# A list scheduler's cost table for TensorE turns and engine overlap is replaced, and the first merge of a block inverse is written for both halves alternately

## The chip, the cores and the metric

The kernel runs on one core of a Trainium2 chip. Its engines are PE (matmul; PEld is its weight load), DVE (vector), ACT (scalar), POOL (GpSimd) and SP (which issues most of the DMAs). They run at the same time; each takes its own instructions strictly in the order in which they stand in its queue. The metric is the device time of one execution in microseconds; the median of three runs before the change is 2573.09 us (2571.34 to 2573.66).

## The reference

One layer of a hybrid decoder, 1024 tokens of width 1024, all in fp32:

```python
x = x + 0.5 * swiglu(rmsnorm(x, ffn1_norm), ffn1_w_gate, ffn1_w_up, ffn1_w_down)
h = rmsnorm(x, mix_norm)
x = x + hybrid_mixer(h, pos, w_in, ...)
x = x + 0.5 * swiglu(rmsnorm(x, ffn2_norm), ffn2_w_gate, ffn2_w_up, ffn2_w_down)
return rmsnorm(x, final_norm)
```

The mixer multiplies `h` by one wide matrix `w_in` and feeds two branches. Branch A is causal dilated sliding-window attention, three groups of four heads with 64 channels, whose outputs are mixed by a softmax over the groups' log-denominators. Branch B is a gated delta rule with eight heads of 128 channels: a short causal convolution and silu on q, k and v, then in chunks

```python
M = where(tri_strict, einsum('bhnid,bhnjd->bhnij', kbeta, kc) * decay, 0.0)
A = M + eye(C)
sol = triangular_solve(A, rhs, left_side=True, lower=True, unit_diagonal=True)
```

and a scan over the chunks that carries a state. Both branches are gated by sigmoids, summed and multiplied by `w_out`.

## The kernel before, in words

**The products.** A wide product is made of three matmuls on operands that are split into a high and a low part of type fp32r (`ff_split`, lines 207 to 218: ACT rounds the high part, L216, and DVE subtracts, L217). These matmuls have 512 (or 256, 272) columns; they are L161 (`proj`, the mixer's projections and the output projection), L274 and L404 (the feed-forward's first half, by a seven-product scheme), L584 (its second half), L697, L801 and L1381. The rest of PE's work is narrow. Transposes through an identity are L201, L877, L928, L975, L1154 and L1226. Full fp32 products, each of which the profile records as two matmuls, are L885, L1129 and the scan's L1185 to L1205. The attention's scores (L864) have 64 rows: the two heads of a pair sit in the upper and the lower half of the array. The smallest are the merges of the triangular inverse, 32 by 32 (L1070, L1075) and 64 by 64 (L1083, L1090).

**The stages.** First feed-forward (to about 715 us), attention (718 to 1046), the combination of the three attention groups mixed with the beginning of head 0 (`combine`, lines 899 to 931, on ACT and DVE, with two transposes L928 for each of eight token tiles and their copy L930), the eight heads of the delta rule (to 1694), the output projection, the second feed-forward and the last norm.

**A head of branch B.** `gdn_keys` projects and convolves k and q (copy out of PSUM L955, convolution L963 on ACT and L965 on DVE, silu L966), and builds the triangular matrix N. `gdn_inverse_blocks` inverts its 32 by 32 diagonal blocks row by row on DVE (L1036 to L1042). `gdn_merge` (from line 1053) joins them: first two 32-blocks into a 64-block, in both halves of the partitions (`quads`: rows 0 to 63 and 64 to 127), over the eight chunks `c`; then two 64-blocks into one of 128. Each join is a product N x T (L1070, L1083), a copy out of PSUM to `W`, and a product U x W (L1075, L1090). `gdn_scan` then runs the eight chunks in turn. Between all of that stand projections of later heads and of the gates, which need nothing of the scan: they are what PE has to fill waits with. Their results leave PSUM through ACT (L942, L955, L828); they have two PSUM buffers (`mm`).

**The end.** The last product of the second feed-forward leaves four PSUM tiles. DVE adds each to its token row (`e4`, L619, tile `acc`), ACT sums the squares (L186), DVE takes the inverse root in twelve small steps that each wait for the one before (`rsqrt_cols`, L123 to L130; tiles `rnv`, `rny`, `rnt`) and writes the row in two halves (L1487, tile `y`), and SP stores them (L1488).

**What sets the order.** The program is built twice. From the first build, `arrange` (from line 1710) simulates the five queues with estimated costs and lays down an order for each; the second build follows it. An instruction's rank is the longest chain of costs behind it. At each step the queue that is free first takes, among the instructions that are ready, the one with the highest rank. `cost` gives for each instruction the time that its queue is held and the time until its result is there; `hop` adds the way from one engine to another. On PE, `form` sorts matmuls into kinds (R wide, T transpose, F full fp32, S scores, Q small squares), and `turn` charges what a change of kind costs. PE goes on with the instruction that follows the last one in program order (`follow`) as long as its rank is within `STAY` of the best.

Of the kernel before, what the change touches and what calls it, by code (L numbers as in the profile page):

```python
# [1055 lines left out]
def gdn_merge(C, N, Tm, Um):  # L1056
# [9 lines left out]
    ps = psum(C, "tM")  # L1066
    W = C.gd.tile([P, NT, 32], F32, name="W", tag="W", bufs=2)
    for lo, hi in quads:
        for c in range(NT):
            nc.tensor.matmul(ps[hi, c * 32:c * 32 + 32], N[lo, c, hi], Tm[lo, c, lo], start=True, stop=True)  # L1070
        nc.vector.tensor_copy(W[hi], ps[hi, :256].rearrange("p (c t) -> p c t", t=32))
    ps = psum(C, "tM")
    for lo, hi in quads:
        for c in range(NT):
            nc.tensor.matmul(ps[hi, c * 32:c * 32 + 32], Um[hi, c, hi], W[hi, c, :], start=True, stop=True)  # L1075
        nc.vector.tensor_copy(Tm[hi, :, lo], ps[hi, :256].rearrange("p (c t) -> p c t", t=32))
        nc.vector.transpose(Um[lo, :, hi], Tm[hi, :, lo])
# [440 lines left out]
class Program:  # L1518
# [118 lines left out]
    def form(self, i):  # L1637
        aps = [a for a in i["ins"] if a["kind"] == "physical_ap"]
        if i["engine"] == "PE":
            if aps[0]["dtype"] == "float32r":  # L1640
                return "R"
            if i.get("is_transpose"):
                return "T"
            return "F" if aps[0]["ap"][0][1] > 64 else "S" if i["outs"][0]["ap"][0][1] > 64 else "Q"
        if i["engine"] == "Activation":
            return {"Exp": "E", "Silu": "U", "Sigmoid": "G", "Ln": "L"}.get(str(i.get("func")).split(".")[-1], "")
        return ""

    def turn(self, a, b, n):

        if a == b:
            return 0
        if b == "S" or b == "Q" or a == "Q":
            return (200 if n < 256 else 300) if a == "S" else 93
        if a == "S":
            return 200 if n < 256 else 300
        return -80 if b == "R" and a in "TF" else 6

# [8 lines left out]
    def cost(self, k):  # L1667
# [15 lines left out]
        if q == 0:  # L1683
            t = {"R": n / 2.4 + 13, "T": 109, "F": 223, "S": 7, "Q": 117 if n > 32 else 63}[self.kind[k]]
            return t, t + 190 + (300 if self.kind[k] == "S" else 0)
        ps = any(self.place[a["memref"]][0] == "PSUM" for a in aps)
# [14 lines left out]
        else:  # L1701
            t = 100 + 0.9 * n + (80 if i["opcode"] == "TensorScalarAffineSelect" else 0)
        return t, t


BACKLOG = 4000
STAY = 1000


# [4 lines left out]
def arrange(prog, pools):  # L1714
# [15 lines left out]
    while stack:  # L1730
        k = stack.pop()
        rank[k] = cost[k][1] if k < n else 0.0
        for c, whole in kids[k]:
            rank[k] = max(rank[k], rank[c] + (cost[k][1] + hop(p.queue[k], p.queue[c]) if whole else 0))
# [21 lines left out]
    while count < n:  # L1756
# [20 lines left out]
        if q == 0 and last[0] is not None:  # L1777
            f = follow.get(last[0])
            if f is not None and not taken[f] and not left[f] and ready[f] <= t and rank[f] >= rank[k] - STAY:
                k = f  # L1780
# [14 lines left out]
        if q == 0:  # L1795
            free0 = clock[q]
            clock[q] -= 80 if p.kind[k] in "TF" else 0
        end = t + cost[k][1]
# [7 lines left out]
        while todo:  # L1806
# [4 lines left out]
            elif not whole:  # L1811
                at = clock[q] if p.queue[c] == q else t
            elif p.queue[c] == q and not p.dma[k]:
                at = clock[q]
            else:
                at = end + hop(q, p.queue[c])
# [51 lines left out]
```

## Time and profile before

| | |
|---|---|
| median of 3 runs | 2573.09 us |
| profiled execution, its own time | 2572.86 us |
| its span, first to last instruction | 2571.1 us |
| granted TensorE clock, mean | 0.991 |
| PE busy | 2508.9 us, 98% |
| DVE busy | 1825.5 us, 71% |
| ACT busy | 983.8 us, 38% |
| PE's share of the chain that ended last | 90% |

How to read the lines that follow. A row of a timeline has the start and the duration in microseconds, the engine, the line, the operation, the tile written and the tiles read, the shapes, and the count of instructions that it merges; in brackets stands how long the engine was idle before and who released it. Matmuls are pipelined, so a row's duration overlaps the next row; what a product costs is the distance between two starts. A row of the waits has the idle time in total, the number of times and the longest one.

### The profile page before, as it was taken

What the parts mean: (1) busy time and instruction counts of PE and PEld (TensorE: products, weight loads), DVE (VectorE), ACT (ScalarE), POOL (GpSimd) and SP (SyncE); (2) the same over time, 40 slices, a digit from 0 to 9 for tenths busy, and PEclk for the clock granted to TensorE, in tenths of its full rate; (3) what the DMA queues carried; (4) which work ended last, traced back from release to release, by engine and by line L of the source; (5) the groups of instructions that cost most, each with busy time, mean ns of one, the idle gap of its engine ahead of it and who ended that gap; (6) DMA issues with size and microseconds to landing.
All of it is one profiled execution on the core that took longest, in us unless ns stands there. A gap on an engine that the chain in (4) does not pass through costs nothing.

```text
span 2571.1 us, 34921 instructions
## 1 busy us (share of the span) xinstructions
PE 2508.9 (98%) x12739; PEld 2074.0 (81%) x12739; DVE 1825.5 (71%) x4059; ACT 983.8 (38%) x1899; POOL 24.4 (1%) x36
## 2 busy tenths in 40 slices
PE   7999999999999999899999999989999999999996
PEld 7788888888888877688888888868888888888885
DVE  8867666768744455888888888546668766667578
ACT  4422332444422336333443335254443333333443
POOL 0000000000000000000000000000000000000000
PEclk9999999999999999999999999999999999999998
DMA  4233224836343331322222213255542223328453
GB/s 159 80 115 114 99 96 168 289 109 203 118 123 94 93 82 52 91 66 64 56 62 56 68 48 81 66 184 193 182 137 91 106 91 115 115 98 301 138 168 111
DMA packets 258172, 301.06 MB, mean 117 GB/s; under 512 B 41840, under 2 KB 175184, under 8 KB 258000
## 3 DMA queue, kind: packets, MB, share of 16 engines
q1 hardware_dynamic: 255696, 292.54, 34.8%
q10 hardware_dynamic: 2304, 6.29, 1.0%
q8 instruction: 100, 1.64, 0.3%
q14 instruction: 72, 0.59, 0.1%
HBM read 217.34 MB, written 75.14 MB: 114 GB/s over the span
## 4 chain that ended last, share of the span: by engine, by line
PE 90%; DVE 6%; DMA 2%; ACT 1%; issue 1%; SPq 0%; DVEq 0%; ACTq 0%
PE mm L161 22%; PE tC L404 13%; PE mm L404 8%; PE tM L404 8%; PE mm L584 4%; PE tC L584 4%; PE tA L161 3%; PE tM L584 3%; PE tA L584 3%; PE mm L697 2%; PE mm L274 2%; PE tC L274 2%; PE tC L1381 2%; PE mm L1381 2%; DMA sgl<-sgbd 1%; PE tA L885 1%
## 5 line engine op out<-in xcount | busy, mean ns | idle before, releaser
L216 ACT CAST fH<-fraw 128x512 fp32r<-128x512 f32 x482 | 289.1, 620 | 463.6 <-PE tM L404 89.4
L217 DVE TENSOR_TENSOR fL<-fraw,fH 128x512 fp32r<-128x512 f32 x482 | 323.0, 689 | 123.8 <-ACT fH L216 118.9
L161 PE MATMUL mm<-hH,fH 128*128 128x512 f32 x896 | 361.5, 410 | 8.7 <-ACT xp L955 5.0
L161 PE MATMUL mm<-hH,fL 128*128 128x512 f32 x896 | 361.0, 405 | 0.0
L161 PE MATMUL mm<-hL,fH 128*128 128x512 f32 x896 | 360.3, 404 | 0.0
L161 PEld LDWEIGHTS mm<-hH,fH 128*128 128x128 f32 x896 | 169.9, 190 | 43.4 <-ACT xp L955 6.2
L161 PEld LDWEIGHTS mm<-hH,fL 128*128 128x128 f32 x896 | 169.7, 190 | 33.3 <-issue 2.3
L161 PEld LDWEIGHTS mm<-hL,fH 128*128 128x128 f32 x896 | 170.1, 190 | 30.3 <-issue 1.7
L404 PE MATMUL mm<-hL,fH 128*128 128x512 f32 x320 | 124.5, 389 | 0.0
L404 PE MATMUL mm<-hH,fL 128*128 128x512 f32 x320 | 121.2, 389 | 0.1
L404 PE MATMUL mm<-hH,fH 128*128 128x512 f32 x320 | 119.0, 389 | 0.0
L576 ACT CAST fH<-hid 128x512 fp32r<-128x512 f32 x154 | 95.0, 617 | 53.1 <-DMA hid<-hd1x 15.8
L577 DVE TENSOR_TENSOR hid<-hid,fH 128x512 fp32r<-128x512 f32 x154 | 104.5, 685 | 5.5 <-ACT fH L576 5.5
L438 DVE TENSOR_TENSOR e<-tM,e 128x512 f32<-128x512 f32 x40 | 26.1, 687 | 79.0 <-PE tM L404 79.0
L216 ACT CAST fH<-hH 128x512 fp32r<-128x512 f32 x68 | 42.3, 622 | 91.3 <-PE tC L584 33.3
L867 DVE CUSTOM_DVE_ANT_0 s<-tC,masks 128x128 f32<-128x128 f32 (+1 forms) x96 | 30.4, 350 | 58.4 <-PE tC L864 35.1
L404 PEld LDWEIGHTS mm<-hH,fL 128*128 128x128 f32 x320 | 60.1, 188 | 13.0 <-DVE fL L217 0.5
L965 DVE SCALAR_TENSOR_TENSOR ka<-xp,cw,ka 128x512 f32<-128x512 f32 x96 | 69.4, 757 | 1.3 <-ACT ka L963 0.8
L404 PEld LDWEIGHTS mm<-hH,fH 128*128 128x128 f32 x320 | 60.0, 188 | 12.6 <-ACT e L408 0.2
L404 PEld LDWEIGHTS mm<-hL,fH 128*128 128x128 f32 x320 | 60.1, 188 | 12.4
L584 PE MATMUL tC<-fH 128*128 128x512 f32 x176 | 68.4, 390 | 0.0
L584 PE MATMUL tC<-fL,fH 128*128 128x512 f32 x176 | 68.2, 389 | 0.0
(402 smaller groups left out, 6200.4 us busy)
## 6 DMA issues: line engine op xcount, KB each, us to landing
fraw<-in_w_in_dram SPq DMA_DIRECT2D x66, 512.0 KB, 3.8
fraw<-in_ffn_w_gate_dram SPq DMA_DIRECT2D x22, 1024.0 KB, 5.2
fraw<-in_ffn_w_up_dram SPq DMA_DIRECT2D x22, 1024.0 KB, 7.2
hL<-in_ffn_w_down_dram SPq DMA_DIRECT2D x8, 1024.0 KB, 6.3
fraw<-in_ffn_w_down_dram SPq DMA_DIRECT2D x8, 1024.0 KB, 6.1
fraw<-in_w_branch_b_dram SPq DMA_DIRECT2D x8, 1024.0 KB, 5.6
fraw<-in_w_out_dram SPq DMA_DIRECT2D x8, 1024.0 KB, 7.3
vb<-xp ACTq DMA_DIRECT2D x48, 128.0 KB, 2.4
```

The source lines that it names most:

```text
L161: nc.tensor.matmul(ps, w, x, start=k == 0 and i == 0, stop=k == kt - 1 and i == 2)
L216: nc.scalar.copy(h, src)
L217: nc.vector.tensor_tensor(out=l, in0=src, in1=h.bitcast(F32), op=ALU.subtract)
L274: nc.tensor.matmul(ps[:, n0:n0 + n], w, x[:, k, c], start=k == 0 and i == 0, stop=k == KT - 1 and i == 2)
L404: nc.tensor.matmul(ps, w, x, start=opens and k == 0 and q == 0, stop=k == 3 and q == 2, skip_group_check=True)
L576: C.nc.scalar.copy(h, v.bitcast(F32))
L577: C.nc.vector.tensor_tensor(out=v, in0=v.bitcast(F32), in1=h.bitcast(F32), op=ALU.subtract)
L584: self.C.nc.tensor.matmul(ps, x[:, m], w, start=p == 0 and i == 0, stop=p == NPAIR - 1 and i == 2)
L697: nc.tensor.matmul(ps[:, :n], h[:, k, b * P:b * P + P], W[k][w], start=k == 0 and i == 0, stop=k == KT - 1 and i == 2)
L867: nc.vector.tensor_tensor_reduce(s[:, h, :nk], ps[h][:, :nk], mask, 1.0, NEG, op0=ALU.add, op1=ALU.max, accum_out=o[:, 128 + h:129 + h])
L965: nc.vector.scalar_tensor_tensor(o, x, w, o, op0=ALU.mult, op1=ALU.add)
L1381: nc.tensor.matmul(ps, mx[:, c], W[k][w], start=i == 0, stop=i == len(seq) - 1)
```

## The change

Three things change; no arithmetic does.

The loops of the first merge in `gdn_merge` are turned: the products of both halves are written alternately over the chunks, all sixteen into the same PSUM tile as before, and the two copies (and the transposes) follow them.

```diff
     ps = psum(C, "tM")
     W = C.gd.tile([P, NT, 32], F32, name="W", tag="W", bufs=2)
+    for c in range(NT):
+        for lo, hi in quads:
+            nc.tensor.matmul(ps[hi, c * 32:c * 32 + 32], N[lo, c, hi], Tm[lo, c, lo], start=True, stop=True)
     for lo, hi in quads:
-        for c in range(NT):
-            nc.tensor.matmul(ps[hi, c * 32:c * 32 + 32], N[lo, c, hi], Tm[lo, c, lo], start=True, stop=True)
         nc.vector.tensor_copy(W[hi], ps[hi, :256].rearrange("p (c t) -> p c t", t=32))
     ps = psum(C, "tM")
+    for c in range(NT):
+        for lo, hi in quads:
+            nc.tensor.matmul(ps[hi, c * 32:c * 32 + 32], Um[hi, c, hi], W[hi, c, :], start=True, stop=True)
     for lo, hi in quads:
-        for c in range(NT):
-            nc.tensor.matmul(ps[hi, c * 32:c * 32 + 32], Um[hi, c, hi], W[hi, c, :], start=True, stop=True)
         nc.vector.tensor_copy(Tm[hi, :, lo], ps[hi, :256].rearrange("p (c t) -> p c t", t=32))
         nc.vector.transpose(Um[lo, :, hi], Tm[hi, :, lo])
```

The scheduler's costs change. The scores get two kinds, S for the upper half and s for the lower, of which the second costs nothing extra behind the first; the table of turns is new; an instruction of DVE or ACT holds its queue 82 or 100 ns less than its result takes, and one that needs the result of another on the same queue waits 40 ns more.

```diff
-        if b == "S" or b == "Q" or a == "Q":
-            return (200 if n < 256 else 300) if a == "S" else 93
-        if a == "S":
-            return 200 if n < 256 else 300
-        return -80 if b == "R" and a in "TF" else 6
+        t = (205 if n < 256 else 305) if a == "S" else 260 if b == "s" else 0
+        if b in "SsQ":
+            return t + (0 if a in "Ss" else 93)
+        if a in "SsQ":
+            return t + (135 if b == "R" else 55) + (100 if a == "Q" else 0)
+        return t + (36 if b == "R" else 9)
...
-        return t, t
+        return t - (0, 82, 100, 0)[q], t
```

And PE stays longer with what it does. Behind a narrow product it goes on with narrow ones up to a difference in rank of `LINGER`, behind a wide one with wide ones up to `STAY`, and takes any of the same sort if the one that follows in program order isn't ready.

```diff
+LINGER = 3000
...
-            if f is not None and not taken[f] and not left[f] and ready[f] <= t and rank[f] >= rank[k] - STAY:
+            wide = p.kind[last[0]] == "R"
+            if f is None or taken[f] or left[f] or ready[f] > t:
+                f = None
+            if f is None or (p.kind[f] == "R") != wide:
+                alike = [(r, c) for r, c in now[0] if not taken[c] and (p.kind[c] == "R") == wide]
+                f = min(alike)[1] if alike else f
+            if f is not None and rank[f] >= rank[k] - (STAY if wide else LINGER):
                 k = f
```

Behind line 1066 the lines of the changed kernel lie two further on: L1075 becomes L1076 (its loops are turned as well), L1083 becomes L1085, L1487 becomes L1489. The new order reaches every queue. On PE, the 11692 matmuls are the same; runs of narrow products between wide ones fall from 462 to 313. The places that matter are shown in the prediction.

More of the change, by code (lines that the diff above doesn't have):

```diff
@@ L1643, in form @@
                 return "T"
-            return "F" if aps[0]["ap"][0][1] > 64 else "S" if i["outs"][0]["ap"][0][1] > 64 else "Q"
+            return "F" if aps[0]["ap"][0][1] > 64 else "Q" if i["outs"][0]["ap"][0][1] <= 64 else "s" if aps[0]["offset"] >= 64 * aps[0]["ap"][0][0] else "S"
         if i["engine"] == "Activation":
@@ L1649, in turn @@
     def turn(self, a, b, n):
-        if a == b:
+        if a == b or a + b == "Ss":
             return 0
-        if b == "S" or b == "Q" or a == "Q":
-            return (200 if n < 256 else 300) if a == "S" else 93
-        if a == "S":
-            return 200 if n < 256 else 300
-        return -80 if b == "R" and a in "TF" else 6
+        t = (205 if n < 256 else 305) if a == "S" else 260 if b == "s" else 0
[4 more added lines that the diff above has]
+        return t + (36 if b == "R" else 9)
     def run(self, a):
@@ L1683, in cost @@
         if q == 0:
-            t = {"R": n / 2.4 + 13, "T": 109, "F": 223, "S": 7, "Q": 117 if n > 32 else 63}[self.kind[k]]
-            return t, t + 190 + (300 if self.kind[k] == "S" else 0)
+            t = {"R": n / 2.4 + 13, "T": 109, "F": 223, "S": n * 0.83 + 106, "s": n * 0.83 + 106, "Q": 117 if n > 32 else 63}[self.kind[k]]
+            return t, t + 190
         ps = any(self.place[a["memref"]][0] == "PSUM" for a in aps)
@@ L1733, in arrange @@
         for c, whole in kids[k]:
-            rank[k] = max(rank[k], rank[c] + (cost[k][1] + hop(p.queue[k], p.queue[c]) if whole else 0))
+            if whole:
+                near = p.queue[k] == p.queue[c] and not p.dma[k]
+                step = cost[k][1] + (hop(p.queue[k], p.queue[c]) if not near else 40 if p.queue[k] in (1, 2) else 0)
+                rank[k] = max(rank[k], rank[c] + (cost[k][0] if near and not p.queue[k] else step))
+            else:
+                rank[k] = max(rank[k], rank[c])
         for d in list(full[k]) + list(after[k]):
@@ L1796, in arrange @@
             free0 = clock[q]
-            clock[q] -= 80 if p.kind[k] in "TF" else 0
         end = t + cost[k][1]
@@ L1813, in arrange @@
             elif p.queue[c] == q and not p.dma[k]:
-                at = clock[q]
+                at = end + 40 if q in (1, 2) else clock[q]
             else:
```

## The prediction

> **What bounds the kernel now.** I read the page, then the busy times by stage, then what the matmul engine PE waits for.
>
> ```profile
> span 2571.1 us, 34921 instructions
> PE 2508.9 (98%) x12739; PEld 2074.0 (81%) x12739; DVE 1825.5 (71%) x4059; ACT 983.8 (38%) x1899; POOL 24.4 (1%) x36
> ```
>
> PE works in 98% of the span, so what counts is what its products cost and where it still waits. The stages of the mixer (attention, combine, eight heads):
>
> ```profile
> 718.00:1046.00 328.00, 326.75 (x1863) 265.03 (x1864) 167.87 (x464) 127.92 (x365) 3.03 (x4) 0.99 0.30 82
> 1046.00:1104.00 58.00, 48.11 (x209) 37.87 (x208) 50.88 (x168) 20.47 (x41) 0.43 (x1) 0.91 0.38 101
> 1104.00:1694.00 590.00, 588.01 (x3623) 485.90 (x3621) 479.53 (x1361) 230.12 (x451) 19.75 (x26) 1.00 0.23 65
> ```
>
> The columns are length, then busy time of PE, weight load, DVE, ACT, POOL, then granted clock. Only in the combine stretch does PE fall short (48.1 of 58.0 us, clock 0.91), and there DVE is 88% busy. In the heads PE is full and DVE 81% busy. PE's waits:
>
> ```profile
> PE tA L201 <- DVE rnv L123: 11.6, 2, 9.5
> PE mm L161 <- ACT yaH L166: 9.7, 1, 9.7
> PE mm L161 <- ACT xp L955: 5.0, 2, 4.9
> PE tA L928 <- DVE cM L916: 2.6, 1, 2.6
> PE tA L928 <- DVE cy L925: 2.4, 2, 2.1
> PE tC L1193 <- DVE xp L952: 1.8, 3, 1.0
> ```
>
> The first stands at the kernel's start, the second where the mixer's buffers turn into those of the output projection, three in the combine, the last in the heads. So a change of order can gain on PE in two ways: cheaper neighbours while it is busy, and shorter waits. A third place is the end, where DVE works alone.
>
> **The change part by part.** The new cost table makes the list scheduler write another order on every queue; the merge's loops are turned. No operation is added or removed. I price neighbours on PE by start-to-start times and count them in the two orders.
>
> *Score products (L864).* They use half the rows of the array; the two heads of a block use different halves. Rows of PE:
>
> ```profile
> 814.67 0.39 PE L161 MATMUL mm<-hL,fH 128*128 128x512 f32 x1
> 814.90 0.40 PE L161 MATMUL mm<-hH,fL 128*128 128x512 f32 x1
> 815.23 0.70 PE L864 MATMUL tC<-ka 64*128 64x256 f32 x4
> 815.86 0.50 PE L161 MATMUL mm<-hL,fH 128*128 128x512 f32 x1
> 816.20 0.39 PE L161 MATMUL mm<-hH,fL 128*128 128x512 f32 x1
> ...
> 816.98 0.70 PE L864 MATMUL tC<-ka 64*128 64x256 f32 x2
> 817.61 0.50 PE L161 MATMUL mm<-hH,fL 128*128 128x512 f32 x1
> ```
>
> A wide product takes 0.23 (814.67 to 814.90). A pair of heads (x4, since each fp32 product has two records) takes 0.63, with 0.10 lost on the way in and 0.11 on the way out: 0.84. A lone head takes the same 0.63 and the same 0.21. Before, 16 heads stand alone among 96, after none: eight visits fewer. Four have 256 columns (0.84); four have 128, which lie between half that and all of it, and I take 0.63: 4 x 0.84 + 4 x 0.63 = **5.9 us**.
>
> *The first merge (L1070, L1075; L1076 after).* On PE, at the merge of head 0 (tM is a PSUM tile, ka here the head's matrix N, Tm and U the inverse blocks, W the first products copied out), before:
>
> ```order
> L1154 MATMUL tA<-ident,vT 128x128 x3
> L1070 MATMUL tM<-Tm,ka 32x32 x8
> L1004 MATMUL tA<-seg,strictR 128x512 x2
> L1154 MATMUL tA<-ident,vT 128x128
> L161 MATMUL mm<-hL_5719,fH 128x512
> L161 MATMUL mm<-hH_5717,fL 128x512
> L161 MATMUL mm<-hH_5718,fH 128x512
> L1070 MATMUL tM<-Tm,ka 32x32 x4
> L1075 MATMUL tM<-W,U 32x32 x8
> L1070 MATMUL tM<-Tm,ka 32x32 x4
> ```
>
> and at the same merge now:
>
> ```order
> L161 MATMUL mm<-hL_5719,fH 128x512
> L1070 MATMUL tM<-Tm,ka 32x32 x16
> L161 MATMUL mm<-hH_5717,fL 128x512
> L161 MATMUL mm<-hH_5717,fH 128x512
> L161 MATMUL mm<-hL_5719,fH 128x512
> L1076 MATMUL tM<-W,U 32x32
> L161 MATMUL mm<-hH_5717,fL 128x512
> L1076 MATMUL tM<-W,U 32x32 x15
> ```
>
> Sixteen products, alternating between two parts of the array, now stand together, where eight of one half and four of the other stood apart. Price of a visit, and of neighbours on different parts:
>
> ```profile
> 1182.33 0.39 PE L161 MATMUL mm<-hL,fH 128*128 128x512 f32 x1
> 1182.65 0.69 PE L1070 MATMUL tM<-Tm,ka 32*32 32x32 f32 x16
> 1183.27 0.50 PE L161 MATMUL mm<-hH,fL 128*128 128x512 f32 x1
> 1183.60 0.40 PE L161 MATMUL mm<-hH,fH 128*128 128x512 f32 x1
> ```
>
> Eight products take 0.62, about 0.063 each and 0.11 around them; the wide neighbours lose 0.09 and 0.10. A visit costs some 0.30 beyond its products. All small square products stand in 76 runs before and 62 after: 14 x 0.30 = **4.2 us**.
>
> ```profile
> 1117.14 0.27 PE L1083 MATMUL tM<-Tm,ka 64*64 64x64 f32 x1
> 1117.15 0.27 PE L1090 MATMUL tM<-U,W 64*64 64x64 f32 x1
> ...
> 1117.76 0.44 PE L975 MATMUL tA<-ident,ka 128*128 128x128 f32 x2
> ```
>
> ```profile
> 1278.68 0.68 PE L1090 MATMUL tM<-U,W 64*64 64x64 f32 x8
> 1279.29 0.50 PE L161 MATMUL mm<-hH,fL 128*128 128x512 f32 x1
> ```
>
> Four products of L1090 alone take 0.61; the four with one of L1083 on another part take 0.62. The second part works for nothing. So of two alternating 32-wide products one is free: 0.031 per neighbour. 228 neighbours alternate after, 23 before: 228 x 0.031 = 7.1. What the 23 bring already:
>
> ```profile
> 1108.15 0.34 PE L1070 MATMUL tM<-Tm,ka 32*32 32x32 f32 x5
> ...
> 1109.07 0.50 PE L161 MATMUL mm<-hH,fL 128*128 128x512 f32 x1
> ```
>
> Here 16 products with two changes of part take 0.92 instead of 16 x 0.063 + 0.11 = 1.12: 0.10 a change, 2.3 in all. Net **4.8 us**. These rows show products that write different PSUM tiles; the alternating ones share one. That is not seen, so the bounds are 7.1 (all free) and -2.3 (none), and I take the first less what is had: the 64-wide rows are the nearest.
>
> The Trainium skill, "TensorEngine Tiling (Array Packing)", section "Restrictions and Gotchas", speaks against this: different row tiles cannot access one PSUM bank at the same time. By it the term is -2.3, and the sum 7 us smaller. That is a rival below.
>
> The cost of the turned loops: the first copy out of PSUM now waits for 16 products instead of 8, and behind it on DVE everything queues. The wide products of L161 cover it on PE (the heads' row has 2 us of idle in 590); uncovered it would be 0.5 us twice a head, 8 us.
>
> *Transposes and full fp32 products.*
>
> ```profile
> 640.43 0.39 PE L584 MATMUL mm<-fL,fH 128*128 128x512 f32 x1
> 640.66 0.60 PE L201 MATMUL tA<-ident,xg 128*128 128x128 f32 x4
> ...
> 641.33 0.40 PE L584 MATMUL tC<-fL,fH 128*128 128x512 f32 x1
> ```
>
> From 640.43 to 641.33 stand two wide products (0.46) and four transposes (0.11 each): a visit costs nearly nothing, 0.01 to 0.02. Their runs fall from 417 to 327: **1.6 us**. PE's busy part together: 5.9 + 4.2 + 4.8 + 1.6 = 16.5.
>
> *Combine.* On ACT, between the copies of the combined attention rows (yT, L930); xp are projections copied out of PE's two mm banks, vT and ka what the convolution makes of them, ce softmax weights. Before:
>
> ```order
> L930 COPY yT<-tA 128x256
> L963 ACTIVATE vT<-xp,cw 128x512 x2
> L930 COPY yT<-tA 128x256
> L966 ACT_TABLE_LOAD
> L966 ACTIVATE vT<-vT 128x512
> L955 COPY xp<-mm 128x512 x2
> ```
>
> and now:
>
> ```order
> L963 ACTIVATE vT<-xp,cw 128x512 x2
> L930 COPY yT<-tA 128x256
> L216 CAST fH<-fraw 128x512
> L913 ACTIVATE ce<-ce 128x12
> L966 ACT_TABLE_LOAD
> L966 ACTIVATE vT<-vT 128x512 x2
> L955 COPY xp<-mm 128x512 x2
> L963 ACTIVATE ka<-xp,cw 128x512 x2
> L930 COPY yT<-tA 128x256
> ```
>
> The copies of L955 that free PE's banks still stand behind an activation that waits for DVE. But between the eight visits of L928 PE's order had 3, 13, 16, 20, 10, 9+0 and 109 wide products, and has 4, 16, 21, 21, 28, 11 and 29 now: never two visits without cover. Before, the waits are 10 us, and the clock falls behind the longest:
>
> ```profile
> 1074.71 0.79 PE L161 MATMUL mm<-hH,fH 128*128 128x512 f32 x1 [4.86 <-ACT xp L955]
> 1075.30 0.63 PE L161 MATMUL mm<-hL,fH 128*128 128x512 f32 x1
> 1075.73 0.63 PE L161 MATMUL mm<-hH,fL 128*128 128x512 f32 x1
> ```
>
> There a wide product takes 0.43 instead of 0.23, until about 1079: 3.5 us. So 13.5 us can go. The Trainium skill, "TensorE: Matmul & The Clock Gate", Part 1, has the clock halved after an idle window of about 3.4 us; the 4.86 agrees, and by it waits in shorter pieces cost only themselves. If every wait slowed the clock once more, the term would be 3.5 smaller, which its lower bound holds. But from the second visit to the last DVE's new order holds, with durations of its rows of before, between 31 us (each overlaps its neighbour) and 46 us (none does) of work, and PE only some 31. Taking DVE at 38, PE still waits 7 us, in pieces, and 2 for ACT. I take **4.5 us** of gain, with bounds of -3 and +12.
>
> *The end.* DVE's last rows; acc are the last four token rows, y the output, the others the norm's chain. Before:
>
> ```order
> L619 SCALAR_TENSOR_TENSOR acc_22018<-tC_22650,acc_22018 128x512
> L130 SCALAR_TENSOR_TENSOR rny_22897<-rnt_22898,rny_22897 128x1
> L128 TENSOR_TENSOR rnt_22898<-rny_22897 128x1
> L129 SCALAR_TENSOR_TENSOR rnt_22898<-rnt_22898,rnv_22896 128x1
> ```
>
> and now:
>
> ```order
> L619 SCALAR_TENSOR_TENSOR acc_22018<-tC_22650,acc_22018 128x512
> L129 SCALAR_TENSOR_TENSOR rnt_22862<-rnt_22862,rnv_22860 128x1
> L130 SCALAR_TENSOR_TENSOR rny_22861<-rnt_22862,rny_22861 128x1
> L128 TENSOR_TENSOR rnt_22862<-rny_22861 128x1
> L129 SCALAR_TENSOR_TENSOR rnt_22862<-rnt_22862,rnv_22860 128x1
> ```
>
> The last sum stood in the third token's chain and stands in the second's (22860). On PE the first of the four groups ended 13 products before the last one, and now ends 33 before, 7.5 us.
>
> ```profile
> 2551.00 0.39 PE L584 MATMUL tC<-fH,hid 128*128 128x512 f32 x1
> 2551.39 0.14 DVE L123 TENSOR_SCALAR rnv<-ssq 128x1 f32<-128x1 f32 x1
> 2553.69 1.41 DVE L1487 SCALAR_TENSOR_TENSOR y<-acc,rny,gB 128x512 f32<-128x512 f32 x2
> 2555.03 0.15 DVE L123 TENSOR_SCALAR rnv<-ssq 128x1 f32<-128x1 f32 x1
> 2565.45 2.73 DVE L1487 SCALAR_TENSOR_TENSOR y<-acc,rny,gB 128x512 f32<-128x512 f32 x4
> ```
>
> A chain takes 2.30 (2551.39 to 2553.69), its y 1.34. Before, four chains and all y follow the last product; DVE ends at 2568.18, 17.2 after it, and the store takes 2.9. Now one chain is done by then and half the next: left are the sum (0.6), five steps (1.0), y (1.3) and two chains with y (7.3), about 11 with the 0.7 until DVE takes the sum. Gain **6.2 us**, bounds 3 and 7.
>
> *Elsewhere.* SP loads three x tiles ahead of the first gate weights, and PE starts with 24 transposes instead of 16: earlier transposes, later weights; 0, bounds of 3 either way in the start's 11.6. At the output projection SP's order is the same (heads' last store, then yal), so the 9.7 stays. The feed-forward stages keep their wide products back to back: 0.
>
> **The rivals.** (A) One PSUM tile cannot be written from two parts at once; the halves take turns: 2546 + 7 = 2553. For it: the rule above, and no row with a shared tile; against: the halves write different partitions. (B) DVE binds: PE's gain in the heads (about 9 us of small products, at 81% DVE) comes back as waits like L1193's, 1 us a head, and the combine gains nothing: 2546 + 8 + 4.5 = 2558.5. Against: the order keeps the cover between the steps of the scan. (C) On the other side: each change of part within a shared tile empties the array, as a visit does with 0.10 and 0.11: 228 x 0.2 = 46, and the 4.8 are gone: 2597, slower. It decides from 0.10 a change. Against: at 1108.15 changes save time. (D) The new turns are no better for the chip than the old, and PE's 16.5 and the combine's 4.5 come to nothing: 2567.
>
> **How the numbers follow.** 16.5 + 4.5 + 6.2 = 27.2. The profiled execution took 2572.86 us, span 2571.1 with 1.8 around it; the median is 2573.09. Forecast 2573.1 - 27.2 = 2546. Chances: forecast 0.58, A 0.20, B 0.13, C 0.04, D 0.05. A measurement of this kernel can tell 0.2% (5.1 us) from no change. Low end: the combine gains 12 and the start 2 (2537); high end: B with a little more (2560). Faster: all but C and some of D: 0.93; same 0.03; slower 0.04.
>
> **What would show it.** Right: L864 only as x4; the x32 records of L1070 in some 0.62 us, not 1.1; waits of L928 and L955 down by a third at least; 14 us, not 20, between the last product and the end. Wrong: alternating rows 0.063 apart (A) or further (C); PE waits of over 10 us in the heads (B); a wait at the start above 15.

## The result and the profile after

| | before | after |
|---|---|---|
| median of 4 runs | 2573.38 us | 2559.51 us |
| profiled execution | 2572.86 us | 2555.95 us |
| its span | 2571.1 us | 2554.2 us |

The ratio is 0.9945 with a 95% interval of 0.9928 to 0.9962: 14 us faster, where 27 were forecast. The direction was right; the time lies inside the stated range, half a microsecond from its upper end. The profiled execution of the changed kernel is the quickest of its four (the others took 2558.8 to 2560.7), and 16.9 us are to be accounted for in it. One execution of no_overlap (below) took 5962 us and is marked slow; without it that kernel's median would be 2583.5 us instead of 2584.0.

The head of the page of the changed kernel, its span and the busy times:

```profile
span 2554.2 us, 34905 instructions
PE 2495.8 (98%) x12739; PEld 2070.5 (81%) x12739; DVE 1771.3 (69%) x4059; ACT 980.0 (38%) x1899; POOL 24.6 (1%) x36
```

PE's share is 98% as before, so the share tells nothing of what was won and lost. The busy times of the combine (first to last L928) and of the heads (to the last head's last transposes), in the columns of the prediction:

```profile
1019.80:1056.50 36.70, 33.24 (x153) 26.23 (x153) 33.49 (x141) 19.56 (x38) 0.00 (x0) 1.00 0.44 125
1056.50:1688.20 631.70, 617.47 (x3768) 508.42 (x3765) 477.36 (x1402) 241.88 (x465) 20.84 (x27) 1.00 0.23 64
```

Where PE was idle for 9.9 of 58.0 us in the combine (1046 to 1104 before) it is now idle for 3.5 of 36.7, at the full clock. In the heads, where it was idle for 2 us in 590, it now is for 14.2 in 631.7. PE's waits in the heads (total, times, longest):

```profile
PE tM L1092 <- DVE W L1087: 3.3, 6, 0.8
PE tM L1085 <- DVE Tm L1078: 2.4, 5, 0.8
PE tC L1187 <- DVE S L1203: 1.8, 3, 0.8
PE tA L1004 <- DVE seg L991: 1.4, 3, 1.1
PE tM L1076 <- issue: 1.1, 2, 0.7
PE tM L1076 <- DVE W L1072: 0.8, 2, 0.5
```

They are new, many and short, none above 1.1 us, and most end with an answer of DVE: between the steps of the merges (L1076, L1085, L1092) and in the scan (L1187).

To see both sides I priced every product of both orders by the prediction's distances (a wide product 0.227, a transpose 0.109, a visit to the small ones 0.30, an alternating neighbour 0.031 less, and so on), summed that for each stage, and set it against the stage's length in the trace. What is left over is the stage's excess: its waits, and the slow steps behind them, where the granted clock is halved. The excess is more than the idle time shown. At the entry to attention two rows of PE are

```profile
714.42 0.39 PE L161 MATMUL mm<-hH,fL 128*128 128x512 f32 x1
716.43 0.50 PE L161 MATMUL mm<-hH,fH 128*128 128x512 f32 x1 [1.63 <-ACT xp L828]
```

2.01 us between the starts are 1.78 more than a wide product, and 1.63 is shown as idle, since a matmul's end is modelled. 0.15 a wait matters where waits are short: in the heads the excess is twice the idle time.

| us | before | after | gain |
|---|---|---|---|
| price of all products | 2487.3 | 2468.9 | 18.4 |
| excess: combine | 13.6 | 4.8 | 8.8 |
| excess: heads | 8.3 | 28.9 | -20.6 |
| excess: entry to attention | 6.6 | 2.1 | 4.5 |
| first product, and excess of the first 100 us | 22.1 | 19.8 | 2.3 |
| excess: attention, output projection, feed-forwards | 13.2 | 16.1 | -2.9 |
| from the last product's start to the end | 20.1 | 13.6 | 6.5 |
| span | 2571.1 | 2554.2 | 16.9 |

(The rows are rounded. The prices are estimates from the prediction's rows, so the split between price and excess is one too.) By these prices PE's products became as much cheaper as forecast and a little more, the end and the combine gained, and the heads gave 20.6 us back.

### The profile page after: what moved, and what is told of

The parts are those of the page before. It is cut to its first block, busy times and chain, and to the rows that moved or that the text cites. A ratio compares the mean times of both kernels' runs of the same rounds, so it can differ in the third digit from the quotient of the medians.

```text
span 2554.2 us, 34905 instructions
## 1 busy us (share of the span) xinstructions
PE 2495.8 (98%) x12739; PEld 2070.5 (81%) x12739; DVE 1771.3 (69%) x4059; ACT 980.0 (38%) x1899; POOL 24.6 (1%) x36
## 4 chain that ended last, share of the span: by engine, by line
PE 85%; DVE 9%; DMA 3%; issue 1%; ACT 1%; SPq 1%; ACTq 0%; DVEq 0%
PE mm L161 18%; PE tC L404 13%; PE mm L404 9%; PE tM L404 8%; PE mm L584 5%; PE tC L584 4%; PE tM L584 4%; PE tA L584 4%; PE tA L161 3%; PE mm L697 2%; PE mm L274 2%; PE tC L274 2%; PE tC L161 2%; PE mm L1383 2%; PE tC L1383 1%; DVE ka L965 1%
## 5 line engine op out<-in xcount | busy, mean ns | idle before, releaser
L161 PE MATMUL mm<-hH,fH 128*128 128x512 f32 x896 | 360.2, 403 | 4.1 <-ACT gt L942 1.6
L161 PE MATMUL mm<-hL,fH 128*128 128x512 f32 x896 | 357.8, 400 | 0.0
L161 PE MATMUL mm<-hH,fL 128*128 128x512 f32 x896 | 352.6, 400 | 0.1
L161 PEld LDWEIGHTS mm<-hH,fH 128*128 128x128 f32 x896 | 168.9, 189 | 37.8 <-ACT gt L942 2.1
L161 PEld LDWEIGHTS mm<-hH,fL 128*128 128x128 f32 x896 | 169.1, 189 | 33.4 <-issue 1.0
L161 PEld LDWEIGHTS mm<-hL,fH 128*128 128x128 f32 x896 | 169.3, 189 | 29.4
L404 PE MATMUL mm<-hH,fL 128*128 128x512 f32 x320 | 123.7, 389 | 0.0
L576 ACT CAST fH<-hid 128x512 fp32r<-128x512 f32 x154 | 94.9, 616 | 14.8 <-DMA hid<-hd1x 9.4
L965 DVE SCALAR_TENSOR_TENSOR ka<-xp,cw,ka 128x512 f32<-128x512 f32 x96 | 74.6, 785 | 17.5 <-ACT ka L963 16.7
L431 DVE TENSOR_TENSOR e<-tC,e 128x512 f32<-128x512 f32 x40 | 27.3, 686 | 66.9 <-PE tC L404 66.9
L584 PE MATMUL mm<-fL,fH 128*128 128x512 f32 x176 | 68.4, 390 | 0.0
```

Of the source, the lines that this page charges most:

```text
L161: nc.tensor.matmul(ps, w, x, start=k == 0 and i == 0, stop=k == kt - 1 and i == 2)
L404: nc.tensor.matmul(ps, w, x, start=opens and k == 0 and q == 0, stop=k == 3 and q == 2, skip_group_check=True)
L431: tt(out=p1[i], in0=ps, in1=p1[i], op=ALU.add)
L576: C.nc.scalar.copy(h, v.bitcast(F32))
L584: self.C.nc.tensor.matmul(ps, x[:, m], w, start=p == 0 and i == 0, stop=p == NPAIR - 1 and i == 2)
L965: nc.vector.scalar_tensor_tensor(o, x, w, o, op0=ALU.mult, op1=ALU.add)
```

## The experiments

Each kernel ran four or five times, merge_only eleven times. The table puts them together; price and excess are as above, from each run's profile. The last column is how many us of the heads had a granted TensorE clock of one half, by the clock records of that trace. "Stay" is the stay rule, "turned" the turned loops, "overlap" the terms of 82, 100 and 40 ns (see overlap_only for what else it holds there), "prices" the costs and turns on PE.

| kernel | what it has of the change | median us | ratio to before, 95% | price | heads' excess | half clock |
|---|---|---|---|---|---|---|
| after_again | all | 2559.3 | 0.9939 (0.9925 to 0.9952) | 2468.9 | 30.7 | 10.2 |
| halves_apart | all, halves unmixed within the order | 2559.3 | 0.9943 (0.9930 to 0.9955) | 2476.0 | 25.1 | 6.8 |
| sched_only | all but turned | 2559.0 | 0.9936 (0.9924 to 0.9949) | 2475.3 | 23.4 | 6.8 |
| old_stay | all but stay | 2562.5 | 0.9953 (0.9941 to 0.9966) | 2468.7 | 34.8 | 17.1 |
| old_turn | all but prices | 2547.5 | 0.9899 (0.9886 to 0.9913) | 2469.8 | 18.6 | 0 |
| no_overlap | all but overlap | 2584.0 | 1.0038 (1.0025 to 1.0052) | 2466.1 | 53.0 | 56.2 |
| overlap_only | overlap | 2543.3 | 0.9883 (0.9870 to 0.9897) | 2475.5 | 12.0 | 0 |
| merge_only | turned | 2573.7 | 1.0000 (0.9991 to 1.0009) | 2482.2 | 15.0 | 3.4 |
| overlap_turn | overlap, prices | 2561.1 | 0.9954 (0.9940 to 0.9967) | 2475.3 | 27.1 | 6.8 |
| overlap_stay | overlap, stay | 2551.0 | 0.9914 (0.9900 to 0.9928) | 2475.2 | 16.8 | 6.8 |
| old_turn_stay | overlap, turned | 2550.1 | 0.9913 (0.9899 to 0.9926) | 2468.7 | 25.4 | 17.1 |
| turn_zero | all, turns at nothing | 2541.5 | 0.9876 (0.9863 to 0.9890) | 2468.6 | 15.0 | 0 |

A product takes about twice as long at half the clock (0.43 us instead of 0.23 for a wide one), so up to half of the last column is part of the excess: 5 of 30.7 us in after_again, 8.5 of 25.4 in old_turn_stay, 28 of 53.0 in no_overlap. Before had none in its heads, the first profile of the changed kernel 3.4 us. Most of the excess of the changed kernel is therefore waiting, but where waits grow the clock adds to them.

My first theory for the heads' waits was the stay rule (theory 1), against the turned loops (3) and the overlap terms (4). Whether alternating products in one PSUM tile overlap was the other question (theory 1 yes, theory 2 no).

**after_again**: the changed kernel, no edit.

> The changed kernel once more, as the ground for the other three on the same chip. Its profile had the heads (from the last L928 to the last head's last transposes) 20.6 us longer than the prices of its products, before 8.3. All theories: 2556 to 2561 us, 0.993 to 0.996 of the kernel before; the waits of L1085, L1092 and L1187 for DVE come back in the heads.

It came as before: heads 633.5 us long, excess 30.7. (The 20.6 us of this expectation, and the 20 of sched_only and old_stay, are the loss against before; set against the prices alone it is the 28.9 of the table above.)

**halves_apart**: the same order of names on every queue; in the second build the loops stand so that each block of sixteen holds the eight products of one half, then those of the other.

```diff
+    pairs = [(c, lo, hi) for c in range(NT) for lo, hi in quads]
+    if not TURNED[0]:
+        pairs.sort(key=lambda x: x[1].start)
...
-    for c in range(NT):
-        for lo, hi in quads:
-            nc.tensor.matmul(ps[hi, c * 32:c * 32 + 32], N[lo, c, hi], Tm[lo, c, lo], start=True, stop=True)
+    for c, lo, hi in pairs:
+        nc.tensor.matmul(ps[hi, c * 32:c * 32 + 32], N[lo, c, hi], Tm[lo, c, lo], start=True, stop=True)
...
+    order = arrange(json.loads(first.to_json_bytes()), pools)
+    TURNED[0] = False
+    nc, _ = build(arrays, order)
```

> The new order on every queue, position for position; only inside each block of sixteen first-merge products (L1070, L1076) the eight of one half now stand ahead of the eight of the other, so 16 neighbours change the part of the array instead of 228. Theory 1 (alternating products overlap although they share a PSUM tile): 212 x 0.031 = 6.6 us more PE time; runs of sixteen take 1.1 us instead of 0.6; 3 to 7 us above the changed kernel, since some of it falls into waits that are there anyway. Theory 2 (one PSUM tile, the halves take turns): no difference within 1 us, and sixteen products take the same time in both.

The first merge of head 0 on PE, in the changed kernel:

```profile
1076.60 0.69 PE L1070 MATMUL tM<-Tm,ka 32*32 32x32 f32 x32
1077.22 0.50 PE L161 MATMUL mm<-hH,fL 128*128 128x512 f32 x1
```

and in halves_apart, where L1070 has become L1072:

```profile
1079.16 1.09 PE L1072 MATMUL tM<-Tm,ka 32*32 32x32 f32 x32
1080.18 0.50 PE L161 MATMUL mm<-hH,fL 128*128 128x512 f32 x1
```

Sixteen products (x32, two records each) take 0.62 us when they alternate and 1.02 when they don't, although they write one PSUM tile: 0.40 for 14 changes of part, 0.029 each, where 0.031 was forecast. Theory 2 falls, and with it rival A. But the median is the same, and the 3 to 7 us more that theory 1 forecast did not come. The price rises by 7.1 us, and the heads' excess falls by 5.6: the heads take 634.7 us with dear products and 633.5 with cheap ones. In these heads, then, cheaper small products bought nothing.

**sched_only**: the changed kernel with the merge's loops of before.

```diff
-    for c in range(NT):
-        for lo, hi in quads:
-            nc.tensor.matmul(ps[hi, c * 32:c * 32 + 32], N[lo, c, hi], Tm[lo, c, lo], start=True, stop=True)
     for lo, hi in quads:
+        for c in range(NT):
+            nc.tensor.matmul(ps[hi, c * 32:c * 32 + 32], N[lo, c, hi], Tm[lo, c, lo], start=True, stop=True)
```

(and the second product likewise.)

> The new scheduler with the merge's loops as before (one half's eight products and its copy, then the other's). By the neighbours in its order PE's products cost 6.4 us more than in the changed kernel. Theory 1 (the waits in the heads come from the scheduler's rules): they stay at some 20 us, and it takes 2563 to 2568. Theory 3 (they come from the turned loops, whose first copy waits for sixteen products instead of eight): they go back to some 8 us, and it takes 2550 to 2556.

The time lies between the two: the same as the changed kernel's. The excess falls only to 23.4, so the turned loops don't make most of the waits (theory 3 falls), and the 6.4 us by which the products are dearer hide in them once more.

**old_stay**: the changed kernel with the old rule of going on.

```diff
-            wide = p.kind[last[0]] == "R"
-            if f is None or taken[f] or left[f] or ready[f] > t:
-                f = None
-            if f is None or (p.kind[f] == "R") != wide:
-                alike = [(r, c) for r, c in now[0] if not taken[c] and (p.kind[c] == "R") == wide]
-                f = min(alike)[1] if alike else f
-            if f is not None and rank[f] >= rank[k] - (STAY if wide else LINGER):
+            if f is not None and not taken[f] and not left[f] and ready[f] <= t and rank[f] >= rank[k] - STAY:
```

> The changed kernel, but PE goes on after a product by the old rule: only with the one that follows in program order, up to 1 us of rank, whatever its kind. Narrow runs 386 instead of 312, yet by neighbours its products cost the same (2468.8 against 2469.0 us), since most of the added runs are transposes. Theory 1 (staying with a kind holds back the product that DVE waits for, and so makes the waits in the heads): the heads' waits fall to about 8 us, 2545 to 2551. Theory 3 (turned loops) or 4 (the overlap term: the order trusts DVE's results too early): waits stay at 20, 2557 to 2562.

Theory 1 falls: the excess is 34.8, and the time 3 us longer. What remained was theory 4, or the new prices. Theory 5 is that the prices of turns make the waits.

**old_turn**: the changed kernel with PE's prices and turns of before. Besides the lines shown, the scores are one kind again, at their old cost, and PE's clock in the plan is set back by 80 ns behind each transpose or full fp32 product, as before.

```diff
...
-        t = (205 if n < 256 else 305) if a == "S" else 260 if b == "s" else 0
-        if b in "SsQ":
-            return t + (0 if a in "Ss" else 93)
-        if a in "SsQ":
-            return t + (135 if b == "R" else 55) + (100 if a == "Q" else 0)
-        return t + (36 if b == "R" else 9)
+        if b == "S" or b == "Q" or a == "Q":
+            return (200 if n < 256 else 300) if a == "S" else 93
+        if a == "S":
+            return 200 if n < 256 else 300
+        return -80 if b == "R" and a in "TF" else 6
...
```

> The changed kernel, but PE's prices and turns as before (one kind of scores, the old table, the 80 ns credit behind transposes); overlap terms, stay rule and turned loops as changed. By neighbours its order costs 2469.8 us on PE against 2469.0 for the changed kernel: the same. Theory 5 (with the new, dearer turns the plan's PE is slow enough to seem covered by DVE, so the plan leaves too little margin and the chip waits in the heads; under the old prices the plan's PE is faster than the chip's and DVE is kept ahead): the heads' excess over the products' price falls from some 25 us to 8, 2536 to 2546. Theory 4 (the overlap term makes the waits): they stay, 2556 to 2562.

11.8 us faster than the changed kernel at the same price of the products. That is theory 5's side, short of its number: the excess falls to 18.6, not to 8, and the time is 1.5 us above its range.

**no_overlap**: the changed kernel without the terms on DVE and ACT.

```diff
-        return t - (0, 82, 100, 0)[q], t
+        return t, t
...
-                at = end + 40 if q in (1, 2) else clock[q]
+                at = clock[q]
```

(and without the 40 in the rank. The rank of chains on PE stays as changed.)

> The changed kernel without the overlap terms on DVE and ACT (82, 100 and 40 ns). By neighbours its order costs 2466.1 us on PE, 2.9 less than the changed one. Theory 4 (trusting DVE's pace makes the waits in the heads): their excess falls to 10 us or less, while combine and end lose some of their gain: 2544 to 2552. Theory 5 (the prices of PE's turns make them): the heads keep 20 us or more, and combine and end lose what the overlap terms gave them, about 6 and 3: 2563 to 2575.

Theory 4 falls the whole way: 24.7 us slower than the changed kernel, slower than the kernel before and 9 us beyond theory 5's range, though its products are the cheapest of all. The excess in the heads is 53.0, of which 25.1 in head 0. Up to half of it is the clock, behind waits of 4.89 us (at the last L928, where the heads begin), 3.17 us and less. The first 100 us of the heads, in the columns as above:

```profile
1061.80:1161.40 99.60, 89.02 (x477) 73.25 (x476) 79.71 (x220) 37.16 (x70) 3.78 (x5) 0.82 0.22 56
```

The mean granted clock there is 0.82, where the changed kernel's heads have 1.00.

**overlap_only**: the kernel before with the overlap terms and the ranks that go with them.

```diff
-        return t, t
+        return t - (0, 82, 100, 0)[q], t
...
-            rank[k] = max(rank[k], rank[c] + (cost[k][1] + hop(p.queue[k], p.queue[c]) if whole else 0))
+            if whole:
+                near = p.queue[k] == p.queue[c] and not p.dma[k]
+                step = cost[k][1] + (hop(p.queue[k], p.queue[c]) if not near else 40 if p.queue[k] in (1, 2) else 0)
+                rank[k] = max(rank[k], rank[c] + (cost[k][0] if near and not p.queue[k] else step))
+            else:
+                rank[k] = max(rank[k], rank[c])
...
-                at = clock[q]
+                at = end + 40 if q in (1, 2) else clock[q]
```

> The kernel before with nothing but the overlap terms on DVE and ACT (and the ranks that go with them); turns, stay rule and merge as before. By neighbours its order costs 2475.3 us on PE, 12.2 less than before's and 6.3 more than the changed one's. Theory 5 (waits come from the new turn prices): the heads wait no more than before, combine and end gain as in the changed kernel: 2541 to 2552, faster than the changed kernel. Theory 4 (waits come from the overlap terms): 2560 to 2568.

This part alone gives 30 us, twice the whole change. It is more than the terms of 82, 100 and 40 ns: the edit also ranks a chain of instructions on PE by the time that each holds the queue, instead of by the time to its result, which is 190 ns or more longer. The changed kernel has this too, and no_overlap kept it; no run has it alone. The gain of the profiled execution: 11.8 by the price, 8.6 in the combine, 6.4 at the end, 4.0 at the entry to attention, 2.1 at the start, less 3.7 in the heads. Its waits in the heads:

```profile
PE tM L1075 <- DVE Tm L1076: 1.0, 3, 0.4
PE tC L1198 <- ACT v L1195: 0.6, 1, 0.6
PE tM L1090 <- PE mm L161: 0.4, 1, 0.4
```

**merge_only**: the kernel before with the turned loops (the edit of the change, first part).

> The kernel before with nothing but the turned loops of the first merge; its scheduler is the old one. By neighbours its order costs 5.3 us less on PE than before's (210 neighbours alternate, 473 narrow runs instead of 461). Theory 1 (alternating products overlap, and before's heads leave PE full, so the gain shows): 2566 to 2570. Theory 2 (no overlap in a shared tile, or the first copy, which waits for sixteen products, takes it back): 2572 to 2578.

No difference, 1.0000 (0.9991 to 1.0009). The price falls by 5.1, but the heads' excess rises from 8.3 to 15.0. Theory 1's overlap is there and its gain isn't.

**overlap_turn**: overlap_only and the new prices and turns (the edit of old_turn undone).

> The kernel before with the overlap terms and the new prices and turns on PE, without the stay rule and the turned loops. By neighbours its order costs the same on PE as that of the overlap terms alone (2475.4 us against 2475.3). Theory 5 (the new prices of turns slow the plan's PE and so take the margin from the heads): the heads' excess rises from the 12 us that the overlap terms alone left to over 20, and it takes 8 to 16 us more than they: 2551 to 2560. Theory 6 (it is the turned loops or the stay rule that do it together with the turns): 2541 to 2547, as the overlap terms alone.

17.8 us slower than overlap_only at the same price: theory 5's side, 1 us above its range, and theory 6 falls. PE is idle in the heads for 11.5 us instead of 3.7, in the same kinds of waits, longer and more of them:

```profile
PE tM L1075 <- DVE Tm L1076: 1.9, 4, 0.6
PE tM L1090 <- issue: 1.5, 5, 0.4
PE tC L1185 <- DVE S L1201: 1.1, 4, 0.4
PE tM L1090 <- DVE W L1085: 1.0, 3, 0.6
```

**overlap_stay**: overlap_only and the stay rule (the edit of old_stay undone).

> The overlap terms and the stay rule, with the old prices of PE and the merge's loops as before. By neighbours 2475.2 us on PE, as the overlap terms alone, with 320 narrow runs instead of 380. If the stay rule is harmless: 2541 to 2546, and the 4 us by which the overlap terms alone beat the kernel with old prices and everything else changed belong to the turned loops. If the stay rule makes waits: 2547 to 2552.

Here the stay rule costs 7.7 us. In the changed kernel it was worth 3.2 (old_stay), and beside overlap and the turned loops 2.6 (old_turn against old_turn_stay). It has no steady price of its own.

**old_turn_stay**: overlap_only and the turned loops.

> The overlap terms and the turned loops, with the old prices of PE and the old stay rule. By neighbours 2468.5 us on PE, 6.8 less than the overlap terms alone, because 230 neighbours alternate. If the turned loops gain what they save on PE: 2535 to 2540. If the first copy, which now waits for sixteen products, and what stands behind it on DVE give it back as waits in the heads: 2542 to 2549, no faster than the overlap terms alone.

6.8 us slower than overlap_only and 1 us above the higher range, although the products are 6.8 cheaper. Of the excess of 25.4, two heads hold 14.8, with waits of up to 1.9 us at L1085. Behind these two waits (1.88 and 1.76 us) the clock is halved:

```profile
1303.63:1310.45 6.82, 6.82 (x33) 5.34 (x31) 6.27 (x13) 3.50 (x7) 0.00 (x0) 0.50 0.16 38
1385.55:1395.79 10.24, 10.24 (x53) 8.69 (x52) 8.33 (x22) 4.01 (x10) 0.00 (x0) 0.50 0.37 101
```

Half of these 17.1 us, an estimate of what the clock costs at most, is 8.5 us, as much as the loss. With the stay rule added (old_turn) 6.8 of it are gone again.

**turn_zero**: the changed kernel with a table of nothings.

```diff
     def turn(self, a, b, n):
...
+        return 0
```

> The changed kernel with every turn on PE priced at nothing, all else as changed, the new costs of the score products included. By neighbours 2468.5 us on PE, 0.5 less than the changed one. Theory 5 (any prices that make the plan's PE faster than the chip's keep DVE ahead and the heads covered, whether the table is right or not): heads' excess at 12 to 19 us instead of 29, 2543 to 2550. Theory 7 (the old table is better because its proportions are): a table of nothings is no better than the new one, 2556 to 2564.

17.8 us below the changed kernel (after_again) and 31 below before, with products 0.3 us cheaper; 1.5 us below theory 5's range. It is the lowest median, but overlap_only's lies within its interval. Theory 7 falls: it is not its proportions that make the old table better, since a table without any does as well or better.

What the prices do is seen in a head. PE's busy time and the others', by 10 us from the beginning of head 2 (its predecessor's last transposes), first two slices and last, in the changed kernel:

```profile
1215.60:1225.60 10.00, 9.28 (x103) 6.69 (x101) 9.87 (x17) 8.71 (x14) 1.27 (x2) 1.00 0.32 105
1225.60:1235.60 10.00, 8.88 (x69) 6.92 (x65) 9.49 (x33) 4.24 (x10) 0.00 (x0) 1.00 0.38 100
...
1285.60:1296.10 10.50, 10.50 (x53) 8.81 (x52) 2.08 (x4) 3.67 (x7) 0.00 (x0) 1.00 0.11 29
```

and in turn_zero:

```profile
1214.70:1224.70 10.00, 9.93 (x106) 7.22 (x104) 9.87 (x17) 8.71 (x14) 1.27 (x2) 1.00 0.31 105
1224.70:1234.70 10.00, 9.87 (x76) 8.24 (x73) 9.45 (x33) 4.53 (x11) 0.00 (x0) 1.00 0.39 107
...
1284.70:1292.50 7.80, 7.80 (x41) 6.58 (x40) 2.10 (x4) 4.13 (x8) 0.00 (x0) 1.00 0.28 72
```

In both, DVE is full for the first 20 us of a head (19.36 and 19.32) and has 2.1 us of work in the last slice. What differs is what PE has to do meanwhile. In those 20 us the changed kernel's order has 34 wide products and waits (excess 3.2); turn_zero's has 42 and hardly waits (0.8). From 60 us behind the head's beginning on, when PE waits for nothing, the changed kernel still has 85 wide products to run (20.5 us), turn_zero 73 (17.8 us); each runs 246 in the head. The tail is equally dense in both, only longer. Heads 1, 3 and 4 repeat it: 33 wide products against 38 to 42 in the first 20 us, with excesses of 2.3 to 3.3 against 0.5 to 1.1. So does the other pair of price tables: overlap_only has 39 or 40 there in heads 1 to 4, overlap_turn 32 to 37. Head 6 does as well (31 in the changed kernel, 38 in turn_zero). Heads 0, 5 and 7 have 53 to 69 in these four kernels and don't show it. So the work that could have covered DVE's stretch is there, and stands later in the head. The merge's rows show it, from the changed kernel:

```profile
1225.57 0.49 PE L161 MATMUL mm<-hH,fH 128*128 128x512 f32 x1
1226.17 0.66 PE L975 MATMUL tA<-ident,ka 128*128 128x128 f32 x4
1226.92 1.16 PE L1131 MATMUL tA<-ka 128*128 128x128 f32 x8
1228.01 1.19 PE L1085 MATMUL tM<-Tm,ka 64*64 64x64 f32 x16
1229.13 1.16 PE L1131 MATMUL tA<-ka 128*128 128x128 f32 x8
1230.57 0.68 PE L1092 MATMUL tM<-U,W 64*64 64x64 f32 x8 [0.28 <-DVE W L1087]
```

and from turn_zero:

```profile
1224.67 0.50 PE L161 MATMUL mm<-hH,fH 128*128 128x512 f32 x1
1225.01 0.40 PE L161 MATMUL mm<-hL,fH 128*128 128x512 f32 x1
1225.24 0.39 PE L161 MATMUL mm<-hH,fL 128*128 128x512 f32 x1
1225.47 0.60 PE L975 MATMUL tA<-ident,ka 128*128 128x128 f32 x4
1226.00 1.14 PE L1085 MATMUL tM<-Tm,ka 64*64 64x64 f32 x16
```

One wide product stands ahead of the join of two 64-blocks (L1085) in the one, three in the other. In the first, a wide product and four transposes take 1.35 us to the next row (1225.57 to 1226.92) and show no idle time; in the second the same take 0.76 (1225.24 to 1226.00).

## Why the prediction was right or wrong, point by point

*PE's busy part, 16.5 forecast, 18.4 by price.* Right as far as is measured. The 18.4 is the prediction's own distances summed over the whole order; PE's busy time, slow steps included, fell by 13.1 us. L864 stands only as pairs (x4). The alternating products overlap at 0.029 instead of 0.031 a change, in one PSUM tile; the bound of 7.1 for "all free" less what was had was the right choice, and rivals A and C fall. The Trainium skill's rule in "TensorEngine Tiling (Array Packing)", section "Restrictions and Gotchas", that row tiles cannot access one PSUM bank at the same time, does not show here as lost time: 0.62 against 1.02.

*Combine, 4.5 forecast, 8.8 measured.* The mechanism was right, the size too small. (The clock was misread, see the last section, and the 3.5 us for it are nearer the length of the slow stretch than its cost, nine steps of 0.20; in the new combine it is full all the same.) The term that was off is DVE's work between the visits, taken at 38 us: the whole stretch now takes 36.7, with DVE busy for 33.5 of it, so PE's share leaves 3.5 us of waits and no slow clock.

*The end, 6.2 forecast, 6.5 measured.* Right by its steps. The last sum and what follows, on DVE:

```profile
2541.07 0.68 DVE L619 SCALAR_TENSOR_TENSOR acc<-tC,acc 128x512 f32<-128x512 f32 x1
2542.62 1.42 DVE L1489 SCALAR_TENSOR_TENSOR y<-acc,rny,gB 128x512 f32<-128x512 f32 x2
2546.26 1.41 DVE L1489 SCALAR_TENSOR_TENSOR y<-acc,rny,gB 128x512 f32<-128x512 f32 x2
2549.90 1.41 DVE L1489 SCALAR_TENSOR_TENSOR y<-acc,rny,gB 128x512 f32<-128x512 f32 x2
```

Three y follow the last product (start 2540.61) instead of four, and DVE ends 10.7 us after it instead of 17.2; 11 was forecast. It comes with the edit of overlap_only, which has 13.7 from the last product to the end, merge_only the old 20.1. no_overlap has 16.5, so the terms on DVE and ACT are not all of it.

*Start and entry to attention, 0 forecast, 2.3 and 4.5 measured.* The start lies within its bound of 3. The entry to attention has no term in the prediction at all. There the wait for L828 fell from 3.7 us to 1.6, and 6.8 us at half clock (717.24 to 724.06 before) with it. In after_again the wait was 2.3 us with 3.4 us at half clock, and 2.3 of the 4.5 were gone again.

*The heads, 0 forecast, 20.6 us lost.* This is the step that failed: "The wide products of L161 cover it on PE (the heads' row has 2 us of idle in 590)", and in rival B "the order keeps the cover between the steps of the scan". A cover was read from before's trace for an order that moved the cover. In the first 20 us of heads 1 to 4 before has 54 to 57 wide products, with an excess of 0.4 us or less, and the changed kernel 33 or 34, with 2.3 to 3.3 us. I had not counted wide products there in the new order. The scan's links lost some of their cover too (L1187, L1200), the merges and what stands beside them lost most. Rival B named this effect, at 0.13 and 8 us. It came at 20.6, beside a gain in the combine that B denied, so the time fell near B's 2558.5 by a different sum. So the time was inside the range by luck: a loss that the forecast had at nothing was offset in part by gains that it had too small.

halves_apart showed that in these heads the cheaper small products bought nothing. turn_zero, old_turn and overlap_turn showed which part of the change takes the cover away: the new prices of PE's turns, for 12 to 18 us in three pairs of kernels with equal price of products. The stay rule and the turned loops have no steady effect, with some 3 us of uncertainty in each difference: 3.2 gained, 7.7 lost and 2.6 gained for the one, 0.3 lost (sched_only, merge_only), 6.8 lost and 3.5 gained (overlap_stay to old_turn) for the other.

*What stays open.* Why dearer turns in the plan move wide products to a later place in the head is argued, not shown: a plan that counts the turns as time already spent on PE sees its waits for DVE covered by them and saves the wide products for later; on the chip a DVE copy that comes a few tenths late then finds PE with nothing to do. A run with later answers from DVE in the plan was not made. Nor was one that changes a single entry of the table. By the prediction's rows a visit to the small squares costs 0.30 us, to transposes 0.01 to 0.02; by the code the old plan charged 0.19 and -0.07, the new one charges 0.33 and 0.045. So the new table is closer in both, yet too dear for transposes, and which entry does the harm is not shown. The two losses of some 7 us with the stay rule and the turned loops go with the clock: overlap_only is at half clock nowhere from the entry to attention to the last head, overlap_stay for 13.7 us, old_turn_stay for 17.1, and half of that is 6.8 and 8.5 us of the 7.7 and 6.8 lost. The mean clocks of their other executions agree (0.995 to 0.997, 0.993 to 0.994, 0.992 to 0.993). Why their orders have the few longer waits that bring this about is open; it may be the luck of a list scheduler.

## What to carry to other kernels

A truer cost in a scheduler's plan need not give a better order: here a table of turns closer to the measured visits was 12 to 18 us worse than the old one or none. The plan's prices decide where free work is spent, and it was spent away from the places where the chip waits. Before counting a gain on a full engine, count in the new order what covers its partner's busiest stretch, piece by piece, and not the idle time of the old trace. When several edits of a scheduler come together, run them apart: here one of them was worth 30 us, another cost 12 to 18, and the third and fourth were worth nothing steady.

## What the runs showed of the hardware

The granted clock can fall behind waits much shorter than the 4.86 us of the prediction. In after_again, at the entry to attention:

```profile
718.47 0.50 PE L161 MATMUL mm<-hH,fH 128*128 128x512 f32 x1 [2.28 <-ACT xp L828]
718.81 0.40 PE L161 MATMUL mm<-hL,fH 128*128 128x512 f32 x1
...
719.83 0.63 PE L161 MATMUL mm<-hH,fL 128*128 128x512 f32 x1
720.26 0.63 PE L161 MATMUL mm<-hH,fH 128*128 128x512 f32 x1
...
723.17 0.39 PE L161 MATMUL mm<-hL,fH 128*128 128x512 f32 x1
```

After 2.28 us of idle the next products still come 0.23 to 0.34 apart until 719.83, 1.4 us behind the wait; then seven come at 0.43. The slow stretch costs about 1.5 us. The clock records tell why it begins late: in each of the fourteen traces all changes of the clock lie whole multiples of 3.41 us apart. The stretch of 3.41 us that holds the wait, and the next one (the clock is the third number from the end):

```profile
716.24:719.65 3.41, 1.18 (x5) 0.99 (x6) 0.68 (x2) 1.80 (x3) 0.00 (x0) 1.00 0.40 90
719.65:723.06 3.41, 3.41 (x10) 2.62 (x9) 3.38 (x7) 0.94 (x4) 0.00 (x0) 0.50 0.55 154
```

The same place in the first profile of the changed kernel, where the wait was 1.63 us and the clock stayed:

```profile
713.57:716.98 3.41, 1.78 (x8) 1.18 (x7) 0.05 (x1) 1.17 (x3) 0.00 (x0) 1.00 0.59 161
716.98:720.40 3.42, 3.42 (x16) 2.81 (x15) 3.39 (x7) 2.49 (x5) 0.00 (x0) 1.00 0.46 123
```

And the kernel before in its combine:

```profile
1065.40:1068.81 3.41, 0.41 (x2) 0.20 (x2) 3.13 (x12) 0.58 (x2) 0.00 (x0) 1.00 0.36 96
1068.81:1072.22 3.41, 0.66 (x2) 0.29 (x2) 3.31 (x9) 2.87 (x4) 0.00 (x0) 0.50 0.30 93
```

PE was idle for 2.23, 1.63 and 3.00 us of the first stretch of each pair. The third pair sets the prediction right. The clock did not fall behind the wait of 4.86 us, which began at 1069.85; it was halved 1.0 us earlier, behind parts of the waits of 2.61 and 2.13 us that fell into one stretch. So waits in shorter pieces don't cost only themselves. In the fourteen traces every stretch at full clock with more than 1.92 us of idle was followed by one at half clock. Below that some were (the least had 0.24 us, in sched_only) and one with 1.92 us was not, so the shown idle time alone doesn't decide. The Trainium skill, "TensorE: Matmul & The Clock Gate", Part 1, gives an idle window of about 3.4 us; the length of the stretches agrees, but here 2.23 us of idle in one sufficed.
